# Running sums of log decays made in the projection stage instead of in the heads, in a hybrid GLA/HGRN2 layer

## The chip, the cores and the metric

One core of one Trainium2 chip. The metric is the device time of one launch in microseconds (us); the kernel before takes 1425.37 us, the median of 3 runs (1425.27 to 1426.08). Engines: TensorE (PE in the profile, PEld its weight loads), VectorE (DVE), ScalarE (ACT), GpSimd (POOL), SyncE (SP, which here only issues DMAs).

## The reference, cut to what matters

For a sequence of 1024 positions and width 1024 a projection `p = x @ w_in` makes queries, keys, values, gates and decays. 4 GLA heads (key width 128, value width 256) and 8 HGRN heads (128, 128) each run a linear attention forward and backward. Per direction and head:

```
g = log_sigmoid(lr @ up + bias) / 16            # GLA
g = log(lb + (1 - lb) * sigmoid(h_f))           # HGRN, key = 1 - f
# chunks of 64 positions:
b = cumsum(g, within the chunk)                 # <- what the change moves
o = (q * exp(b)) @ S + masked(q k exp(b_i - b_j)) @ v
S = exp(b_last) * S + (k * exp(b_last - b))^T @ v
```

The outputs of both directions are added, normalised per head, gated, projected (`w_branch_gla`, `w_branch_hgrn`), merged by two sigmoid gates, multiplied by `w_out`, and layer-normed with the residual. All of it is float32.

## The kernel before, in words

The program is written in a tile framework that orders the instructions of each engine itself: it plans with a modelled duration for every instruction and DMA, takes work in the order of the program unless something else is ready earlier, and lets instructions under `high_priority` go first. Each engine and each DMA queue then runs its list strictly in that order. Buffers are tiles with a tag; a tag has a fixed number of buffers, and a new tile waits until the last reader of the tile before it in that buffer is done.

Three stages follow each other; matrix products are made of float32 halves (`split`, lines 88 to 92: a rounded copy on ScalarE, the rest on DVE).

*Stage one* (`dense`, line 1224, about 0 to 711 us) makes all projections by a scheme with seven half-size products in place of eight (`seven`, line 999; the sums of line 1012 run on DVE at high priority). Narrow jobs (TensorE lines 975) make transposed 128-wide pieces: first eight of kind `decay` (`narrow_job`, line 1175), then four `swish`, then `scale` and `copy`; the wide jobs (line 988) make values and gates. While job n runs, the weights of job n + 1 are loaded on SP into `raw` tiles (5 buffers), summed and split. A `decay` job ends with four tiles of 128 x 512 (`h`, 14 buffers), one per head and half: line 1200 makes the key on POOL, line 1202 takes the log on ScalarE in place, line 1203 stores it to the DRAM tensor `logs`. In eight narrow jobs `gla_logs` (line 1159) follows: it makes the GLA logs of one head and direction, 128 x 1024, in two `raw` tiles, the last step on DVE (line 1172), and stores them too. All stores of stage one go out on POOL's queue (`store`, line 920).

*Stage two* (`heads`, line 1471, about 705 to 1213 us) runs the 12 heads in the order of SEQUENCE. `decays` loads a head's logs for both directions into FB and FF (line 1401, 128 x 1024 each, 2 buffers each, on SP). `scaled` (line 1415) makes with a scan on DVE (line 1422) the running sums of the logs into PB and PF (2 buffers each). The scan multiplies the sum so far by `runs`, which is 1.0 everywhere and 0.0 at each 64th position, so that it starts again at every half chunk; direction 1 runs from the right. Then: the last sums of each half chunk are copied to `logs`, a small tile (line 1433), one half is shifted by them (line 1437), two exponentials write FF/FB (line 1440) and PF/PB (line 1441), and these become the scaled key (line 1443) and query (line 1442). `attend` (line 1491) makes the scores (TensorE line 382, masks on DVE lines 392 to 395, with a scratch tile `sq`), transposes the scaled keys (line 540), runs the states (lines 566 and 1568), and ends with the output products `po` (line 566), which read the scaled queries PF and PB and the values `v`. So FF/FB are read until a head's transposes, PF/PB and `v` until its last output products. Projections that the heads don't need (`merge_gate`, `gla_branch`, TensorE line 1364) are given to TensorE between the heads' own products.

*Stage three* (about 1213 to 1425 us) makes the branch projection, the merge and the output; the diff does not touch it.

Of the kernel before, what the change touches and what calls it, by code (L numbers as in the profile page):

```python
# [13 lines left out]
ALU = mybir.AluOpType  # L14
AX = mybir.AxisListType

P = 128
# [857 lines left out]
class Fast(Layer):  # L875
# [283 lines left out]
    def gla_logs(self, h, d):  # L1159

        nc = self.nc
        f, m = self.t("raw"), self.t("raw")
        bias = self.prm[:, 4 * d + h : 4 * d + h + 1]
        for n in range(2):
            o = slice(512 * n, 512 * n + 512)
            ps = self.bank()
            nc.tensor.matmul(ps, self.ups[:, d, P * h : P * h + P], self.lr[:, o], start=True, stop=True)
            nc.scalar.activation(f[:, o], ps, AF.Abs, bias=bias)
            nc.vector.tensor_scalar(out=m[:, o], in0=ps, scalar1=bias, scalar2=0.0, op0=ALU.add, op1=ALU.min)
        nc.scalar.activation(f, f, AF.Exp, scale=-1.0)  # L1170
        nc.scalar.activation(f, f, AF.Ln, bias=1.0)
        nc.vector.tensor_tensor(out=f, in0=m, in1=f, op=ALU.subtract)
        self.store(self.logs[2 * h + d], f)

    def narrow_job(self, kind, at, w):
        nc = self.nc
        late = []

        def out(i, j, _, c, psum):
            s = c if kind == "copy" and not psum else self.h()  # L1180
            col = slice(512 * j, 512 * j + 512)
            if kind == "scale":
                nc.scalar.mul(s, c, QSCALE)
            elif kind != "copy":
                nc.scalar.activation(s, c, AF.Sigmoid)
            elif psum:
                nc.scalar.copy(s, c)
            if kind == "swish":
                nc.vector.scalar_tensor_tensor(out=s, in0=c, scalar=QSCALE, in1=s, op0=ALU.mult, op1=ALU.mult)
            if kind == "decay":  # L1190
                late.append((i, col, s))
            else:
                self.store((self.ks if kind == "copy" else self.qs)[at + i][:, col], s)

        self.seven(self.narrow_product(w, self.xs), 1, out, at == 0 and kind == "decay")
        for i, col, s in late:
            n = HGRN_HEADS * i + at
            o, b = self.omlb[:, n : n + 1], self.lb[:, n : n + 1]
            k = self.h()
            nc.gpsimd.tensor_scalar(out=k, in0=s, scalar1=self.nomlb[:, n : n + 1], scalar2=o, op0=ALU.mult, op1=ALU.add)  # L1200
            self.store(self.ks[GLA_HEADS + n][:, col], k)
            nc.scalar.activation(s, s, AF.Ln, scale=o, bias=b)
            self.store(self.logs[2 * (GLA_HEADS + at) + i][:, col], s)

    def wide_job(self, kind, columns, w):
# [18 lines left out]
    def dense(self):  # L1224
        nc = self.nc
        self.slot, self.stage_one = T, True
        self.counts = {"raw": 5, "s": 3, "w": 8, "h": 14}
        heads = GLA_HEADS + HGRN_HEADS
        self.qs = self.dr.tile([heads, P, T], F32, name="qs")
        self.ks = self.dr.tile([GLA_HEADS + 2 * HGRN_HEADS, P, T], F32, name="ks")  # L1230
        self.logs = self.dr.tile([2 * heads, P, T], F32, name="logs")
        self.sigs = self.dr.tile([16, P, T], F32, name="sigs")
        self.staged = {}
        jobs = []
        for h in range(HGRN_HEADS):
            jobs.append(("decay", h, (H_FF + P * h, H_FB + P * h)))
        for h in range(0, HGRN_HEADS, 2):
            jobs.append(("swish", GLA_HEADS + h, (H_Q + P * h, H_Q + P * h + P)))
        for h in range(0, GLA_HEADS, 2):
            jobs.append(("scale", h, (A_Q + P * h, A_Q + P * h + P)))  # L1240
            jobs.append(("copy", h, (A_K + P * h, A_K + P * h + P)))
        narrow = len(jobs)
        for start, kind, n in ((A_GATE, "gate", 4), (H_GATE, "gate", 4), (A_V, "v", 4), (H_I, "v", 4)):
            for b in range(0, n, 2):
                jobs.append((kind, None, (start + 256 * b, start + 256 * (b + 1))))

        def block(column):
            halves = []
            for n in range(2):
                r = self.t("raw", (P, 4, 256))  # L1250
                nc.sync.dma_start(out=r, in_=self.io["ww"][WIDE.index(column)][:, 4 * n : 4 * n + 4, :])
                halves.append(r)
            return halves

        def prepare(n):
            kind, at, columns = jobs[n]
            if n < narrow:
                return self.pair_sums(self.pair_loads(self.io["wn"], *(NARROW.index(c) for c in columns)))
            a, b = block(columns[0]), block(columns[1])
            return self.sums(a[0], a[1], b[0], b[1], 256)  # L1260

        nc.sync.dma_start(out=self.prm, in_=self.io["prm"])
        ready = self.load_x(lambda: self.pair_loads(self.io["wn"], *(NARROW.index(c) for c in jobs[0][2])))
        self.lower_bounds()
        self.nomlb = self.t("nomlb", (P, 16))
        nc.vector.tensor_scalar(out=self.nomlb, in0=self.omlb, scalar1=-1.0, scalar2=None, op0=ALU.mult)
        for n, (kind, at, columns) in enumerate(jobs):
            ahead = prepare(n + 1) if n + 1 < len(jobs) else None
            if n < narrow:
                self.narrow_job(kind, at, ready)  # L1270
            else:
                self.wide_job(kind, columns, ready)
            if n == narrow - 9:
                self.low_product()
            elif n >= narrow - 8 and n < narrow:
                self.gla_logs(*divmod(n - narrow + 8, 2))
            ready = ahead
        for i in range(self.STARTED, self.BEGUN):
            self.merge_half(i)
# [115 lines left out]

    def decays(self, n):

        fs = []
        for d in (1, 0):
            f = self.t("FB" if d else "FF")  # L1400
            self.nc.sync.dma_start(out=f, in_=self.logs[2 * n + d])
            fs.insert(0, f)
        return fs

    def key(self, n):
        k = self.t("K")
# [5 lines left out]
        self.nc.sync.dma_start(out=q, in_=self.qs[n])  # L1412
        return q

    def scaled(self, q, k, f, unit, d, index):

        nc = self.nc
        pr = self.t("PB" if d else "PF")
        last = 0 if d else 63
        seg = lambda a: a.rearrange("p (s j) -> p s j", j=64)  # L1420
        step = -1 if d else 1
        nc.vector.tensor_tensor_scan(  # L1422
            out=pr[:, ::step],
            data0=self.runs,
            data1=f[:, ::step],
            initial=0.0,
            op0=ALU.mult,
            op1=ALU.add,
        )
        logs = self.t(f"logs{d}", (P, NT, 2))  # L1430
        ends = self.t(f"ends{d}", (P, NT, 2))
        flat = lambda a: a.rearrange("p c h -> p (c h)")
        nc.vector.tensor_copy(out=flat(logs), in_=seg(pr)[:, :, last])
        nc.vector.tensor_reduce(out=self.minp[:, index : index + 1], in_=flat(logs), axis=AX.X, op=ALU.min)
        nc.scalar.activation(flat(ends), flat(logs), AF.Exp, scale=unit)
        half = pr.rearrange("p (c h j) -> p c h j", h=2, j=64)[:, :, d, :]
        nc.vector.tensor_tensor(
            out=half, in0=half, in1=logs[:, :, d].unsqueeze(2).to_broadcast([P, NT, 64]), op=ALU.subtract
        )
        nc.scalar.activation(f, pr, AF.Exp, scale=-unit)  # L1440
        nc.scalar.activation(pr, pr, AF.Exp, scale=unit)
        nc.vector.tensor_tensor(out=pr, in0=pr, in1=q, op=ALU.mult)
        nc.vector.tensor_tensor(out=f, in0=f, in1=k, op=ALU.mult)
        return pr, f, ends
# [26 lines left out]
    def heads(self):  # L1471
        nc = self.nc
        self.oa = self.dr.tile([KC, P, T], F32, name="oa")
        self.oh = self.dr.tile([KC, P, T], F32, name="oh")
        self.ua = self.dr.tile([KC, P, T], F32, name="ua")
        self.runs = self.t("runs")
        nc.vector.memset(self.runs, 1.0)
        nc.vector.memset(self.runs.rearrange("p (s j) -> p s j", j=64)[:, :, 0], 0.0)
        for n, name in enumerate(self.SEQUENCE):
            (self.gla_front if name[0] == "A" else self.hgrn_front)(int(name[1]))  # L1480
            if n == 0:
# [210 lines left out]
    def run(self):  # L1692
        of = lambda *names: [f"{name}{k}" for name in names for k in range(4)]
        with ExitStack() as ctx:
# [3 lines left out]
            with ExitStack() as kept:  # L1698
                self.keep_x = self.pool(kept, "keepx")
                with ExitStack() as c:  # L1700
                    self.tops = self.pool(c, "tops")
                    self.stage(c, "p0", [["raw"], ["s"], ["w"], ["h"]])
                    self.dense()
                with ExitStack() as c:
                    self.stage(
# [6 lines left out]
                            ["Sf", "sq"],  # L1712
                            ["V"],
                            ["FB", "FF"],
                            ["runs"],
                            ["PB", "PF"],
                            ["v"],
                            ["A", "KT", "Sb"],
# [92 lines left out]
```

## Time and profile before

| | |
|---|---|
| median of 3 runs | 1425.37 us |
| the profiled execution | 1426.49 us |
| its span, first to last instruction | 1424.8 us |
| granted TensorE clock, mean over the span | 0.975 of full |
| busy: PE, PEld, DVE, ACT, POOL | 1339.6 (94%), 1152.1 (81%), 862.4 (61%), 670.6 (47%), 182.9 (13%) us |
| chain that ended last, shares | PE 71%, DMA 10%, DVE 7%, ACT 5%, issue 5% |

The profile is one execution; times inside it are us from the first instruction. "Busy" counts the time in which an engine executes something. A timeline row is: start, duration, engine, line of the kernel, operation, written tile <- read tiles, shapes, how many such instructions in a row; in brackets the time the engine stood idle just before, and what ended that. `sc`, `po`, `st`, `proj` and `bank` are PSUM tiles.

### The profile page before, as it was taken

To read this page: it belongs to the slowest core of one execution; us is meant where nothing else is said; L and a number is where in the kernel's file an instruction comes from. 1 tells how busy PE (TensorE), PEld (TensorE's weight loads), DVE (VectorE), ACT (ScalarE), POOL (GpSimd) and SP (SyncE) were. 2 spreads that over 40 slices of the span, in tenths; PEclk is the share of its full clock that TensorE was granted. 3 is DMA by queue.
4 is the path that set the end of the run, shared out by engine and by line. 5 is a ranking of instruction groups with operands and counts; after the bars stand their busy time and mean duration, and the time that the engine had idled before them with its cause. 6 is when DMAs were issued, how large, how long until landed. Compare 5 with 4: busy or idle time off the path is not lost.

```text
span 1424.8 us, 21066 instructions
## 1 busy us (share of the span) xinstructions
PE 1339.6 (94%) x8009; PEld 1152.1 (81%) x8009; DVE 862.4 (61%) x1410; ACT 670.6 (47%) x1190; POOL 182.9 (13%) x270
## 2 busy tenths in 40 slices
PE   7999979999999999999989999987889999799996
PEld 5888858877799999999968877765677888577885
DVE  8755645776566665544463666766788443665544
ACT  6656565774533333222244565556676454653100
POOL 1234350111111011011100010111110100000011
PEclk9999989999999999999999999998899999899998
DMA  7444342333433332332473454355565331865431
GB/s 274 140 148 167 129 151 101 135 138 111 154 131 108 107 102 99 99 114 104 144 278 121 139 185 166 109 177 177 178 231 212 104 112 60 294 231 169 150 103 55
DMA packets 83153, 210.45 MB, mean 148 GB/s; under 512 B 10656, under 2 KB 10656, under 8 KB 80992
## 3 DMA queue, kind: packets, MB, share of 16 engines
q1 hardware_dynamic: 68368, 160.48, 33.1%
q0 software_dynamic: 14672, 48.51, 9.0%
q8 instruction: 65, 1.06, 0.3%
q14 instruction: 48, 0.39, 0.1%
HBM read 137.65 MB, written 71.30 MB: 147 GB/s over the span
## 4 chain that ended last, share of the span: by engine, by line
PE 71%; DMA 10%; DVE 7%; ACT 5%; issue 5%; POOL 0%; SPq 0%; DVEq 0%; POOLq 0%; ACTq 0%
PE bank L988 22%; PE bank L975 16%; PE proj L1364 12%; PE bank L1636 6%; PE po L566 4%; PE st L566 3%; DMA raw<-in_dram 3%; PE sc L382 2%; DMA wraw<-in_dram 2%; PE bank L1304 2%; DMA g<-ua 2%; DMA oa<-ot 1%; PE sc L540 1%; DVE PF L1422 1%; DMA hraw<-oa 1%
## 5 line engine op out<-in xcount | busy, mean ns | idle before, releaser
L975 PE MATMUL bank<-xP,w 128*128 128x512 f32 x1344 | 315.5, 395 | 13.6 <-DVE h L1012 7.0
L988 PEld LDWEIGHTS bank<-w,xP 128*128 128x128 f32 x2688 | 323.5, 192 | 1.1 <-DVE w L92 0.8
L988 PE MATMUL bank<-w,xP 128*128 128x256 f32 x2688 | 323.6, 283 | 0.3 <-DVE w L92 0.3
L975 PEld LDWEIGHTS bank<-xP,w 128*128 128x128 f32 x1344 | 255.1, 190 | 71.4 <-DVE h L1012 8.4
L1364 PE MATMUL proj<-x,hw 128*128 128x512 f32 x576 | 147.1, 399 | 0.1
L92 DVE TENSOR_TENSOR w<-s,w 128x512 fp32r<-128x512 f32 (+1 forms) x96 | 84.0, 877 | 76.3 <-ACT w L91 76.1
L91 ACT CAST w<-s 128x512 fp32r<-128x512 f32 (+1 forms) x96 | 72.6, 760 | 121.7 <-PE bank L988 78.7
L91 ACT CAST w<-raw 128x512 fp32r<-128x512 f32 (+1 forms) x90 | 65.1, 732 | 128.4 <-PE bank L988 67.0
L1364 PEld LDWEIGHTS proj<-x,hw 128*128 128x128 f32 x576 | 104.9, 188 | 21.9 <-issue 0.7
L1364 PE MATMUL proj<-xP,hw 128*128 128x512 f32 x360 | 97.8, 411 | 6.3 <-DVE hw L92 5.5
L1364 PE MATMUL bank<-oh,hw 128*128 128x512 f32 x384 | 93.1, 401 | 9.9 <-ACT hw L91 4.8
L1529 POOL TENSOR_TENSOR rs<-msall,mhalf 128x4 f32<-128x4 f32 (+1 forms) x32 | 43.0, 1343 | 447.2 <-DVE msall L1528 444.5
L1364 PEld LDWEIGHTS bank<-oh,hw 128*128 128x128 f32 x384 | 72.4, 192 | 30.5 <-ACT hw L91 7.9
L1012 DVE TENSOR_TENSOR h<-bank,h 128x512 f32<-128x512 f32 x96 | 65.8, 687 | 45.9 <-PE bank L988 33.4
L92 DVE TENSOR_TENSOR w<-raw,w 128x512 fp32r<-128x512 f32 (+1 forms) x90 | 75.3, 843 | 29.6 <-ACT w L91 29.6
L1364 PEld LDWEIGHTS proj<-xP,hw 128*128 128x128 f32 x360 | 67.2, 193 | 21.9 <-DVE hw L92 6.6
L1012 DVE TENSOR_TENSOR h<-h,bank 128x512 f32<-128x512 f32 x65 | 44.4, 684 | 53.9 <-PE bank L988 28.7
L92 DVE TENSOR_TENSOR hw<-hraw,hw 128x512 fp32r<-128x512 f32 x64 | 43.8, 687 | 42.5 <-ACT hw L91 42.5
L1566 ACT ACTIVATE V<-st,ends 128x128 f32<-128x128 f32 (+1 forms) x168 | 58.6, 414 | 22.5 <-PE st L566 22.2
L566 PE MATMUL st<-v,KT 128*128 128x128 f32 (+1 forms) x336 | 61.0, 323 | 2.6 <-ACT KT L541 1.4
L1304 PE MATMUL bank<-xP,w 128*128 128x512 f32 x216 | 52.3, 404 | 8.0 <-ACT xP L91 6.6
L91 ACT CAST hw<-hraw 128x512 fp32r<-128x512 f32 x64 | 39.6, 618 | 36.9 <-PE proj L1364 25.6
(194 smaller groups left out, 2008.2 us busy)
## 6 DMA issues: line engine op xcount, KB each, us to landing
raw<-in_dram SPq DMA_DIRECT2D x82, 256.0 KB, 3.2
hraw<-in_dram SPq DMA_DIRECT2D x68, 256.0 KB, 3.5
raw<-in_dram SPq DMA_DIRECT2D x33, 512.0 KB, 3.7
ks<-h POOLq DMA_DIRECT2D x40, 256.0 KB, 3.1
K<-ks SPq DMA_DIRECT2D x20, 512.0 KB, 4.9
logs<-h POOLq DMA_DIRECT2D x32, 256.0 KB, 3.7
gated<-h POOLq DMA_DIRECT2D x32, 256.0 KB, 2.7
vd<-h POOLq DMA_DIRECT2D x32, 256.0 KB, 2.7
```

What stands on the lines that cost most here:

```text
L91: nc.scalar.copy(hi, raw)
L92: (lo_engine or nc.gpsimd).tensor_tensor(out=lo, in0=raw, in1=hi.bitcast(F32), op=ALU.subtract)
L382: mm = lambda out, l, r: nc.tensor.matmul(out, l, r, start=True, stop=True)
L566: self.nc.tensor.matmul(out, l, r, start=(i == 0), stop=(i == len(terms) - 1))
L975: self.nc.tensor.matmul(out[0], a[i][:, k, :], b[k][:, j, :], start=(n == 0 and not more), stop=(n == len(terms) - 1), skip_group_check=True,)
L988: self.nc.tensor.matmul(out[c // 2][:, 256 * (c % 2) : 256 * (c % 2) + 256], b[k][:, j, P * c : P * c + P], a[i][:, k, :], start=(n == 0 a ...
L1012: nc.vector.tensor_tensor(out=to[n], in0=one[n], in1=two[n], op=op)
L1304: self.nc.tensor.matmul(ps, w.both[a][:, k, :], xs[k][:, b, :], start=(m == 0), stop=(m == len(terms) - 1))
L1364: nc.tensor.matmul(ps, parts[k][a], self.plain[k, n][:, b, :], start=(m == 0), stop=(m == len(terms) - 1))
L1529: nc.gpsimd.tensor_tensor(out=rs[:, cs], in0=ms, in1=self.mhalf[:, cs], op=ALU.pow)
L1566: nc.scalar.mul(new, u, ends[:, c, near : near + 1])
L1636: nc.tensor.matmul(pss[m], y[:, k, rows], self.wo[k, n][:, j, part], start=(i == 0), stop=(i == len(terms) - 1))
```

## The change

The scan moves to where the logs are made. In stage one a new function `sum_up` runs it in place, 512 columns at a time, on DVE, between the making of the logs and their store; `runs` becomes a tile of 128 x 512 of stage one, made at its start, and `h` has 13 buffers in place of 14. The DRAM tensor `logs` now holds running sums. In stage two the load goes straight into PB and PF, and FB and FF are first written by the exponentials.

```
@@ gla_logs
         nc.vector.tensor_tensor(out=f, in0=m, in1=f, op=ALU.subtract)
+        self.sum_up(f, d)
         self.store(self.logs[2 * h + d], f)
+
+    def sum_up(self, f, d):
+        for n in range(f.shape[1] // 512):
+            u = f[:, 512 * n : 512 * n + 512][:, :: -1 if d else 1]
+            self.nc.vector.tensor_tensor_scan(out=u, data0=self.runs, data1=u, initial=0.0, op0=ALU.mult, op1=ALU.add)
@@ narrow_job
             nc.scalar.activation(s, s, AF.Ln, scale=o, bias=b)
+            self.sum_up(s, i)
             self.store(self.logs[2 * (GLA_HEADS + at) + i][:, col], s)
@@ dense
-        self.counts = {"raw": 5, "s": 3, "w": 8, "h": 14}
+        self.runs = self.t("runs", (P, 512))
+        nc.vector.memset(self.runs, 1.0)
+        nc.vector.memset(self.runs.rearrange("p (s j) -> p s j", j=64)[:, :, 0], 0.0)
+        self.counts = {"raw": 5, "s": 3, "w": 8, "h": 13}
@@ decays
-            f = self.t("FB" if d else "FF")
-            self.nc.sync.dma_start(out=f, in_=self.logs[2 * n + d])
-            fs.insert(0, f)
+            pr = self.t("PB" if d else "PF")
+            self.nc.sync.dma_start(out=pr, in_=self.logs[2 * n + d])
+            sums.insert(0, pr)
@@ scaled
-    def scaled(self, q, k, f, unit, d, index):
-        pr = self.t("PB" if d else "PF")
+    def scaled(self, q, k, pr, unit, d, index):
+        f = self.t("FB" if d else "FF")
-        step = -1 if d else 1
-        nc.vector.tensor_tensor_scan(
-            out=pr[:, ::step], data0=self.runs, data1=f[:, ::step],
-            initial=0.0, op0=ALU.mult, op1=ALU.add,
-        )
@@ heads
-        self.runs = self.t("runs")
-        nc.vector.memset(self.runs, 1.0)
-        nc.vector.memset(self.runs.rearrange("p (s j) -> p s j", j=64)[:, :, 0], 0.0)
@@ run: the pools of stage one and two
-                    self.stage(c, "p0", [["raw"], ["s"], ["w"], ["h"]])
+                    self.stage(c, "p0", [["runs"], ["raw"], ["s"], ["w"], ["h"]])
...
-                            ["runs"],
```

## Rows read from the trace of the kernel before

**Rows 1.** Busy times by stretch: from:to, length, PE, PEld, DVE, ACT, POOL, clock, DMA
```profile
45.00:240.00 195.00, 187.07 (x800) 152.89 (x799) 105.38 (x159) 113.61 (x167) 65.44 (x100) 0.97 0.40 140
240.00:392.00 152.00, 144.81 (x643) 118.38 (x643) 99.29 (x145) 96.57 (x129) 19.95 (x37) 0.98 0.38 133
392.00:711.00 319.00, 319.00 (x2648) 318.58 (x2647) 177.31 (x203) 91.07 (x116) 34.52 (x64) 1.00 0.33 111
711.00:734.00 23.00, 17.78 (x77) 14.12 (x76) 12.85 (x11) 5.12 (x8) 2.16 (x4) 0.96 0.68 260
734.00:880.00 146.00, 144.91 (x918) 118.76 (x918) 95.18 (x191) 80.96 (x174) 9.46 (x8) 0.98 0.45 159
880.00:1100.00 220.00, 191.22 (x1222) 153.24 (x1220) 161.10 (x318) 137.53 (x304) 25.08 (x18) 0.94 0.53 184
1100.00:1213.00 113.00, 112.57 (x713) 96.05 (x714) 50.84 (x112) 56.13 (x142) 6.41 (x4) 1.00 0.28 96
```

**Rows 2.** Line 1422's own row: count, ns least/median/most, first and last start
```profile
L1422 DVE TENSOR_TENSOR_SCAN PB<-runs,FB x12: 2260/2286/2292, 726.4 to 1129.8; 128x1024 f32<-128x1024 f32 x12
```

**Rows 3.** Timeline of TensorE, waits behind DVE in the heads
```profile
733.62 5.41 PE L1364 MATMUL proj<-xP,hw 128*128 128x512 f32 x12 [4.37 <-DVE hw L92]
...
959.23 1.11 PE L540 MATMUL sc<-ident,FB 128*128 128x128 f32 x4 [4.01 <-DVE sq L393]
...
997.74 0.71 PE L540 MATMUL sc<-ident,FB 128*128 128x128 f32 x4 [4.01 <-DVE sq L393]
...
1028.32 0.24 PE L382 MATMUL sc<-PB,FB 128*64 128x64 f32 x1 [1.82 <-DVE sq L393]
```

**Rows 4.** Timeline of DVE at two of the scan pairs
```profile
954.33 2.28 DVE L1422 TENSOR_TENSOR_SCAN PB<-runs,FB 128x1024 f32<-128x1024 f32 x1
...
958.78 0.40 DVE L393 TENSOR_TENSOR sq<-sc,m 128x256 f32<-128x256 f32 x1
...
1054.54 2.28 DVE L1422 TENSOR_TENSOR_SCAN PB<-runs,FB 128x1024 f32<-128x1024 f32 x1
```

**Rows 5.** Busy times by stretch, four short ones behind TensorE's waits
```profile
734.00:740.00 6.00, 6.00 (x17) 4.71 (x17) 6.00 (x21) 5.26 (x9) 0.00 (x0) 0.60 0.77 279
960.00:970.00 10.00, 8.41 (x40) 6.29 (x38) 9.93 (x22) 8.84 (x16) 0.70 (x1) 0.80 0.54 177
998.00:1008.00 10.00, 8.39 (x47) 7.64 (x46) 9.81 (x24) 8.01 (x18) 0.69 (x1) 0.66 0.38 121
1062.00:1075.00 13.00, 8.16 (x72) 6.72 (x70) 12.62 (x28) 9.47 (x17) 1.48 (x1) 0.87 0.77 269
```

**Rows 6.** Timeline of SP: a load of logs, a load of values
```profile
924.53 0.40 SPq L1401 DMA_DIRECT2D FB<-logs  x1
...
954.82 0.32 SPq L1322 DMA_DIRECT2D v<-vd  x1
```

**Rows 7.** DMA issues: what, queue, count, KB each, median us to landing
```profile
FB<-logs SPq DMA_DIRECT2D x12, 512.0 KB, 4.0
FF<-logs SPq DMA_DIRECT2D x12, 512.0 KB, 6.0
```

**Rows 8.** Groups of DVE instructions by form: count, busy us, mean ns, idle
```profile
L1442 DVE TENSOR_TENSOR PF<-PF,Q 128x1024 f32<-128x1024 f32 x12 | 14.6, 1217 | 0.8 <-ACT PF L1441 0.8
...
L1437 DVE TENSOR_TENSOR PF<-PF,logs 128x512 f32<-128x512 f32 x12 | 8.2, 679 | 0.0
```

**Rows 9.** Narrow jobs from 240: TensorE timeline, then a line of DVE's waits
```profile
316.19 4.16 PE L975 MATMUL bank<-xP,w 128*128 128x512 f32 x17 [1.22 <-DVE w L92]
...
388.08 5.49 PE L975 MATMUL bank<-xP,w 128*128 128x512 f32 x12 [2.98 <-DVE h L1012]
...
DVE s L938 <- DMA raw<-in_dram: 12.7, 4, 5.2
```

**Rows 10.** A decay job: DVE behind the logs; line 1200's own row
```profile
159.46 0.69 DVE L92 TENSOR_TENSOR w<-s,w 128x512 fp32r<-128x512 f32 x1 [3.95 <-ACT w L91]
...
L1200 POOL TENSOR_SCALAR h<-h,nomlb,omlb x32: 766/770/1783, 56.4 to 209.6; 128x512 f32<-128x512 f32 x32
```

More of the change, by code (lines that the diff above doesn't have):

```diff
@@ L1396, in decays @@
     def decays(self, n):
-        fs = []
+        sums = []
         for d in (1, 0):
-            f = self.t("FB" if d else "FF")
-            self.nc.sync.dma_start(out=f, in_=self.logs[2 * n + d])
-            fs.insert(0, f)
-        return fs
+            pr = self.t("PB" if d else "PF")
+            self.nc.sync.dma_start(out=pr, in_=self.logs[2 * n + d])
+            sums.insert(0, pr)
+        return sums
     def key(self, n):
@@ L1413, in query @@
         return q
-    def scaled(self, q, k, f, unit, d, index):
+    def scaled(self, q, k, pr, unit, d, index):
         nc = self.nc
-        pr = self.t("PB" if d else "PF")
+        f = self.t("FB" if d else "FF")
         last = 0 if d else 63
         seg = lambda a: a.rearrange("p (s j) -> p s j", j=64)
-        step = -1 if d else 1
-        nc.vector.tensor_tensor_scan(
[L1423 to L1428, printed above, removed]
-        )
         logs = self.t(f"logs{d}", (P, NT, 2))
```

## The prediction

> **What bounds the kernel now.** I read the page first, then busy times by stage, then TensorE's idle times, then what VectorE (DVE) runs just before each of them. By the page TensorE is busy 94% of the span; the 6% it is not are what a change off TensorE can win or lose. The stage table [rows 1] says where they lie. In the first stage's narrow jobs (45 to 392 us) TensorE is idle 7.9 + 7.2 = 15.1 us, in its wide jobs (392 to 711) not at all, at the border of the stages (711 to 734) 5.2 us, in the first heads (734 to 880) 1.1 us, in the middle heads (880 to 1100) 28.8 us. There DVE is busy 161 of 220 us, 73%, more than in the narrow jobs (54% and 65%).
>
> The 24 scans of line 1422 take 2.28 us each (the row is of the PB half; the PF half is alike) [rows 2], 24 x 2.28 = 54.8 us. They come in pairs, one pair a head. TensorE's long waits in the heads [rows 3] are mostly waits for something that stands behind such a pair in DVE's queue. The clearest: the pair runs from 954.33, `sq` of line 393 follows at 958.78 [rows 4], and TensorE, which needs the bank that `sq` reads, starts at 959.23 after 4.01 us of idleness. `sq` belongs to the head before; it waits for no scan by data, only by place. Rows 3 has the same at 997.74 and 1028.32, and at 733.62, where both heads' scans stand ahead of a weight split. Behind the pair of 1054.54 DVE's queue is nearly full until 1075 [rows 4, 5], with 4.84 us of TensorE idleness.
>
> After such idleness TensorE runs slow for a while: of its two levels (1.2 and 2.4 GHz) it is granted the lower for part of each stretch that follows, mean 0.60, 0.80, 0.66 and 0.87 [rows 5].
>
> **Part 1: the scans leave the heads.** Stalls that go: 4.37 + 4.01 + 4.01 + 1.82 [rows 3] and of the 4.84 at 1062 to 1075 about 4.4, the length of the pair: 18.6 us. Lost clock that goes with them [rows 5]: 6 x 0.40 + 10 x 0.20 + 10 x 0.34 + 13 x 0.13 = 9.5 us. Together 28 us. The other pairs lie beside dense TensorE work (734 to 880, and after 1100) and free nothing there. The memset of `runs` in line 1477 goes too; nothing waits for it for long, 0.
>
> What is late next is the part's own new wait. The load of the logs now lands in PF/PB, not in FF/FB. FF/FB are free once a head's transposes are done, so the old load goes out some 30 us ahead of its scan (issued at 924.53, scan at 954.33). PF/PB are read until the head's last output products; only then can the load go out, about when the load of `v`, which is freed by the same products, goes out today, 954.82 [rows 6]. From issue to landing it takes a median of 4.0 us for FB and 6.0 for FF [rows 7], where the pair of scans took 4.5. So the decays of a head are ready 0 to 1.5 us later than now, in ten of twelve heads (the first two find free buffers). The copies of line 1433, the four exponentials on ScalarE and the products behind them wait for it, and whatever stands behind those on the two in-order queues. Cover: DVE has the previous head's mask products, `ss`, `gate` and `A` to do (it is 9.93 of 10 us busy at 960 to 970 [rows 5]). On SP, weight loads, stores of `ot` and K and Q loads stand behind a load that waits. Bounds: 0, and 10 x 1.5 = 15 us; I take the middle, 8, because the two medians lie on both sides of 4.5. Heads: -28 + 8 = -20.
>
> **Part 2: the scans enter the first stage.** No row shows a scan of 512. DVE operations of 512 and 1024 columns take 679 and 1217 ns [rows 8], 0.56 of the long one; a scan of 512 is then between 1.14 (half) and 2.28 us (if length did not matter), and nearest 0.56 x 2.28 = 1.27; I take 1.25. There are 8 x 2 in the low-rank decays and 32 in the jobs of kind decay: 48 x 1.25 = 60 us on DVE.
>
> Low-rank decays (240 to 392): 2.5 us more behind line 1172 in each of 8 blocks, DVE from 99 to 119 of 152 us. Queued behind: weight splits and `h` sums, for which TensorE waits; on the POOL queue the store leaves 2.5 us later, with the stores of `qs` and `ks` behind it, and the `raw` buffer comes free 2.5 us later for the next weight load on SP. Four times in this region DVE stands waiting for a weight load, 12.7 us in all [rows 9], 3.2 each: those blocks hide their scans. Of the other four, TensorE already waits right behind two: 1.22 us at 316.19, 2.98 at 388.08 [rows 9]. Four exposed blocks make 10 us, all eight 20, none 0; since the sums and splits are issued at high priority and may be put ahead of the scans, I take 7.
>
> Decay jobs (the first eight, in 45 to 240): four scans a job, 5 us, behind four Lns of ScalarE. They fall on a DVE that is idle 3.95 us at this place [rows 10] and 46% of the stretch [rows 1]; 1 to 2 us a job spill into the next idle times. Bounds 0 and 8 x 2 = 16; I take 0, since TensorE is busy 187 of 195 and the weights are split a job ahead. The log store on POOL waits up to 5 us longer; behind it stands the next job's line 1200, whose engine is busy 65 of 195 us. One `h` buffer less (13 of 14): a job uses 11 and they are free after their store, 0; without that cover the `h` sums wait out one store, about the 4.0 us of rows 7, a job. The memsets of the shorter `runs` run while the first loads are under way, 0. Wide jobs: TensorE 319.00 of 319 busy, nothing changes.
>
> One rule speaks against the move. In rows 10, line 1200 on POOL takes 770 ns as a rule and up to 1783 where a DVE operation with two SBUF inputs runs. The Trainium skill ("SBUF — State Buffer", section "SBUF: two separate sides") says why: such a DVE operation and a GpSimd operation that reads SBUF take an exclusive lock, and one waits for the whole of the other; the trace's extra 1 us agrees. A scan has two SBUF inputs. In the heads POOL reads little; here line 1200 is next door. I count 0, as POOL is on no path; the case in which it counts is a rival.
>
> **Sum.** -20 + 7 + 0 = -13 us. The profiled execution took 1426.49 us (span 1424.8, 1.7 around it), 1.1 above the median of 1425.37. 1426.5 - 13 - 1.1 = **1412 us**.
>
> **Rivals.** (a) *The load takes the scans' place.* If DVE's copies of line 1433 stand in its queue ahead of the previous head's work, DVE waits for the whole load: ten heads x (0.4 issue [rows 6] + 6.0) = 64 us in place of 10 x 4.5 = 45, +19; no stall goes but that of the border (4.4 + 2.4 of clock), +7 in the first stage: +19, **1445**, slower. It decides from a landing later than the ready work lasts. For it: the order is planned before the run, with a modelled load, and load and products now follow each other. Against: DVE has ready work then, and the decays are needed only a head later.
> (b) *The first stage pays in full.* All eight blocks expose their scans: +20 - 20, **1425**, no change. For it: the waits at 316.19 and 388.08. Against: four idle times of 3.2 us.
> (c) *All of it pays.* The loads hide (8), the blocks hide (7), and half of the other 14.6 us of idleness at 880 to 1100 goes with a shorter queue (7): **1390**. For it: the waits there are of one loop, head after head, that DVE stands in. Against: some of them wait for ScalarE and for loads.
> (d) *The lock counts.* A scan in each job meets a POOL operation and waits its 0.77 us out, 8 x 0.77 = 6 us, all on TensorE's path: 1412 + 6 = **1418**. So far the trace lets POOL and DVE collide without TensorE waiting.
> That the change doesn't do what it says I leave out: each scan starts again at every 64 columns, so 512 at a time are the same sums, and 24 scans must leave the heads.
>
> **How the numbers follow.** Forecast 45% (its own range 1403 to 1421), (a) 20%, (b) 17%, (c) 14%, (d) 4%. No change means within 0.2%, 1422.5 to 1428.2, about what a measurement can tell. Of (b) 5 points fall below, 9 inside, 3 above. Faster: 45 + 14 + 4 + 5 = 68%; same 9%; slower 20 + 3 = 23%. The range 1394 to 1436 leaves out about half of (c) and two thirds of (a), 20%.
>
> **What would show it.** Right: no scan after 711; TensorE goes on at about 729 and not 733.6; no wait of 4 us on `sq` of line 393; granted clock near 1.00 at the places of rows 5; TensorE idle at 880 to 1100 down from 28.8 to about 15; scans of about 1.25 us; 240 to 392 some 7 us longer. Loads of PB and PF go out with or after the last output products and line 1433 follows a landing. Wrong: DVE idle before line 1433, waiting for a load, for more than 1 us a head (a); narrow jobs longer by over 15 us, with TensorE waiting behind line 1172 (b). A new order in which the heads no longer interleave as now would undo the working as a whole.

## The result, and the profile after

The changed kernel takes 1408.15 us, median of 4 runs (1404.65 to 1414.26), beside 1425.72 of the kernel before in the same session: ratio 0.9871, 95% interval 0.9826 to 0.9916. The forecast was 1412. A second set of runs, on another chip, gave 0.9854 (0.9822 to 0.9885). Times and ratios are of the fast runs alone: a run of 4618.48 us, of the version with 13 `h` buffers below, is left out. The profiled execution took 1407.21 us, span 1405.5, mean clock 0.978. The busy times by stretch of the kernel after, to set beside [rows 1]:

```profile
45.00:240.00 195.00, 186.91 (x793) 152.55 (x792) 137.84 (x185) 110.74 (x163) 68.94 (x99) 0.96 0.39 137
240.00:392.00 152.00, 145.87 (x660) 119.20 (x658) 118.06 (x165) 101.53 (x136) 18.91 (x35) 1.00 0.37 130
711.00:734.00 23.00, 22.37 (x110) 18.68 (x109) 6.64 (x16) 5.01 (x9) 2.70 (x5) 1.00 0.69 252
880.00:1100.00 220.00, 199.89 (x1276) 160.57 (x1275) 142.35 (x313) 142.37 (x312) 15.49 (x18) 0.95 0.58 197
```

DVE's work has moved as counted: +32 and +19 us in the two narrow stretches, less in the stretches behind 711. TensorE is idle 20.1 us at 880 to 1100 in place of 28.8. But the work no longer stands in the same microseconds, so the heads have to be cut by their own ends: from the last product of line 988 to the first of line 848, behind the last head. First the kernel before, then after:

```profile
710.90:1221.50 510.60, 471.34 (x2960) 386.12 (x2958) 324.54 (x645) 281.62 (x629) 45.13 (x36) 0.97 0.46 163
```

```profile
714.00:1203.80 489.80, 464.66 (x2961) 381.66 (x2959) 276.19 (x621) 281.74 (x630) 30.56 (x36) 0.98 0.48 166
```

The heads, border included, are 20.8 us shorter: TensorE's idle time falls from 39.26 to 25.14 (-14.1), and the same products (2960 and 2961 records) take 6.7 us less of TensorE's time. Stage one ends 3.1 us later, and what lies behind line 848 takes 1.6 less: +3.1 - 20.8 - 1.6 = -19.3, the difference between the spans.

The scans after, by line, are to be set beside [rows 2] (count, least/median/most ns, first and last start):

```profile
L1180 DVE TENSOR_TENSOR_SCAN h<-runs,h x32: 1197/1200/1226, 69.8 to 217.8; 128x512 f32<-128x512 f32 x32
L1180 DVE TENSOR_TENSOR_SCAN raw<-runs,raw x16: 1199/1208/1224, 249.8 to 391.7; 128x512 f32<-128x512 f32 x16
```

None starts after 391.7. Of [rows 3], the border and the three waits on `sq` have no successor. TensorE goes on at the border at 730.93 (it was 733.62), and at 946.52 it starts the transposes with no wait, since `sq` has been made at once. TensorE's timeline first, then DVE's of the same head:

```profile
730.93 0.73 PE L1375 MATMUL proj<-xP,hw 128*128 128x512 f32 x2 [0.63 <-ACT hw L91]
...
946.52 0.60 PE L540 MATMUL sc<-ident,FB 128*128 128x128 f32 x4
```

```profile
945.99 0.42 DVE L393 TENSOR_TENSOR sq<-sc,m 128x256 f32<-128x256 f32 x1
...
949.16 0.17 DVE L1435 COPY logs<-PB 128x16 f32<-128x16 f32 x1
...
955.70 0.17 DVE L1435 COPY logs<-PF 128x16 f32<-128x16 f32 x1 [2.42 <-DMA PF<-logs]
```

The last row is the new wait: line 1435 (1433 before) copies the ends of the sums once the load has landed. The loads go out on SP with `v`, as they had to:

```profile
945.42 0.32 SPq L1412 DMA_DIRECT2D PB<-logs  x1
946.28 0.32 SPq L1333 DMA_DIRECT2D v<-vd  x1
946.71 0.36 SPq L1412 DMA_DIRECT2D PF<-logs  x1
```

The clock at the four places of [rows 5] is not what it was to be:

```profile
734.00:740.00 6.00, 6.00 (x28) 4.97 (x27) 0.99 (x3) 1.01 (x2) 0.00 (x0) 1.00 1.03 404
960.00:970.00 10.00, 8.86 (x49) 5.76 (x49) 6.54 (x11) 8.89 (x21) 0.00 (x0) 0.75 0.88 328
998.00:1008.00 10.00, 9.82 (x71) 9.15 (x71) 3.50 (x8) 5.01 (x15) 0.00 (x0) 0.77 0.75 254
1062.00:1075.00 13.00, 13.00 (x79) 11.42 (x78) 5.57 (x12) 7.68 (x23) 0.57 (x1) 0.92 0.43 143
```

Only the border is at 1.00; two of the others rose, by 0.11 and 0.05, and one fell by 0.05. Part of this is other work, as the heads run up to 18 us earlier; DVE, 97 to 100% busy at these places before, has room at all four. In the heads TensorE now waits mostly for ScalarE (waited for: us in total, times, longest):

```profile
PE st L566 <- ACT V L1565: 5.1, 7, 1.6
PE po L1539 <- ACT ot L1545: 3.8, 4, 2.3
PE proj L1375 <- ACT hw L91: 3.2, 3, 1.6
```

### The profile page after: what moved, and what is told of

It reads as the page before. It is cut to its first block, busy times and chain, and to the rows that moved or that the text cites. A ratio compares the mean times of both kernels' runs of the same rounds, so it can differ in the third digit from the quotient of the medians.

```text
span 1405.5 us, 21115 instructions
## 1 busy us (share of the span) xinstructions
PE 1333.9 (95%) x8009; PEld 1150.1 (82%) x8009; DVE 867.5 (62%) x1434; ACT 670.9 (48%) x1190; POOL 172.6 (12%) x270
## 4 chain that ended last, share of the span: by engine, by line
PE 74%; DMA 11%; ACT 6%; DVE 5%; issue 3%; POOL 1%; SPq 0%; POOLq 0%; DVEq 0%; ACTq 0%
PE bank L988 22%; PE bank L975 16%; PE proj L1375 13%; PE bank L1635 6%; PE po L566 5%; PE st L566 3%; PE sc L382 2%; DMA raw<-in_dram 2%; PE bank L1315 2%; DMA PF<-logs 2%; DMA hraw<-in_dram 2%; PE bank L1375 2%; DMA g<-ua 1%; DMA g<-sigs 1%; DMA oa<-ot 1%
## 5 line engine op out<-in xcount | busy, mean ns | idle before, releaser
L1375 PE MATMUL proj<-xP,hw 128*128 128x512 f32 x360 | 94.3, 402 | 2.0 <-ACT hw L91 1.6
L1528 POOL TENSOR_TENSOR rs<-msall,mhalf 128x4 f32<-128x4 f32 (+1 forms) x32 | 28.4, 887 | 441.2 <-DVE msall L1527 434.8
```

What stands on the lines that cost most here:

```text
L1375: nc.tensor.matmul(ps, parts[k][a], self.plain[k, n][:, b, :], start=(m == 0), stop=(m == len(terms) - 1))
L1528: nc.gpsimd.tensor_tensor(out=rs[:, cs], in0=ms, in1=self.mhalf[:, cs], op=ALU.pow)
```

## The experiments

The theory: the 24 scans cost time by their place, ahead of the previous head's masks in DVE's queue. The main rival: they cost by DVE's time, wherever they stand. Each ratio is to runs of the kernel before on the same chip, with its 95% interval; versions that ran on different chips are compared by these ratios. "heads" is the stretch of one profile from the last product of line 988 to the first of line 848; before it is 510.6 us.

**The load early again.** The sums are loaded into FF/FB and the query's exponential is the first to write PF/PB:

```
-            pr = self.t("PB" if d else "PF")
-            self.nc.sync.dma_start(out=pr, in_=self.logs[2 * n + d])
+            f = self.t("FB" if d else "FF")
+            self.nc.sync.dma_start(out=f, in_=self.logs[2 * n + d])
... in scaled: copies and shift on f, then
-        nc.scalar.activation(f, pr, AF.Exp, scale=-unit)
-        nc.scalar.activation(pr, pr, AF.Exp, scale=unit)
+        nc.scalar.activation(pr, f, AF.Exp, scale=unit)
+        nc.scalar.activation(f, f, AF.Exp, scale=-unit)
```

> The changed kernel, but the sums are loaded into FF/FB, which come free some 30 us ahead, and PF/PB are first written by the exponential of the query side. Theory (the load that now waits for the last output products is a cost that is still being paid, DVE's 13.9 us of waits for PF's load): about 1400 us, and no wait of line 1435 for a load. Rival one (the loads are covered, the waits fall beside other work): the changed kernel's 1408. Rival two (both exponentials now run one after the other behind PF/PB's release, and ScalarE becomes the late one): 1412 or more.

Measured: 1396.64 us, 0.9778 (0.9756 to 0.9800), heads 481.5. It is the version that beats both kernels. Run again beside two others below:

> e1_prefetch once more, unchanged, beside the two above on one chip: 0.976 to 0.980 if its gain over the changed kernel is real; 0.984 to 0.988 if it was the scatter of one chip.

1398.0 us, 0.9772 (0.9741 to 0.9804), heads 486.0: the gain over the changed kernel is real, its two ratios being 0.008 to 0.010 higher than these two, 11 to 14 us. My reason for it fell, though. DVE waits longer for loads than in the changed kernel. The changed kernel's waits, and then this one's:

```profile
DVE logs L1435 <- DMA PF<-logs: 13.9, 8, 3.2
```

```profile
DVE logs L1435 <- DMA FB<-logs: 19.7, 6, 6.0
DVE logs L1435 <- DMA FF<-logs: 13.4, 8, 4.7
```

What counts is when it waits: 25.0 of these 33.1 us lie before 888, a stretch in which TensorE misses nothing (144.88 of 146 us busy at 734 to 880). In the middle heads DVE's timeline shows the copies of the head that the changed kernel copies at 949.16 and 955.70 some 32 us earlier, 5 of them from an earlier end of stage one, in the head before and away from its end:

```profile
917.11 0.18 DVE L1435 COPY logs<-FB 128x16 f32<-128x16 f32 x1
...
923.58 0.18 DVE L1435 COPY logs<-FF 128x16 f32<-128x16 f32 x1 [0.84 <-DMA FF<-logs]
```

**Scans that nobody needs, in the changed kernel.** Two of 512 columns a head and direction, of the loaded sums, into a tile that nothing reads:

```
+        junk = self.t("junk", (P, 512))
+        for n in range(2):
+            u = pr[:, 512 * n : 512 * n + 512][:, :: -1 if d else 1]
+            nc.vector.tensor_tensor_scan(out=junk, data0=self.ones, data1=u, initial=0.0, op0=ALU.mult, op1=ALU.add)
```

> The changed kernel with two scans of 512 columns per head and direction put back into the heads, on the loaded sums, into a scratch that nobody reads (1.2 us each, 58 us of DVE in all; the output is unaffected). Theory (what cost before was the scans' place in DVE's queue, ahead of the previous head's work): the gain of the heads goes, about 1425 us, with TensorE waiting again behind DVE operations of lines 392 to 395. Rival (what cost was that the exponentials needed the scans' result): nobody needs these, so 1408 to 1412.

1412.55 us, 0.9875 (0.9852 to 0.9898), where my theory said 1425: DVE has the 58 us in the heads again (163 of 220 us busy at 880 to 1100, more than before), and most of the gain stays. The timeline of DVE shows why: these scans become ready only with the late landing, so the masks go ahead of them:

```profile
905.23 0.42 DVE L393 TENSOR_TENSOR sq<-sc,m 128x256 f32<-128x256 f32 x1
...
909.68 1.22 DVE L1433 TENSOR_TENSOR_SCAN junk<-ones,PF 128x512 f32<-128x512 f32 x1 [2.22 <-DMA PF<-logs]
```

By the ratios they cost 1 to 3 us; in its profile, an execution 4 us above the median, the heads are 502.0, 12 longer. The size is not settled between the two.

**The scans at the old place, their result needed by nobody.** The early-load version with 24 scans of 1024 columns from FF/FB into PF/PB, which the exponential then overwrites:

```
+        nc.vector.tensor_tensor_scan(
+            out=pr[:, ::step], data0=self.runs2, data1=f[:, ::step], initial=0.0, op0=ALU.mult, op1=ALU.add
+        )
```

> The kernel of the early loads (sums made in stage one, loaded into FF/FB), with the 24 scans of 1024 columns put back where they were, from FF/FB into PF/PB; the exponential then writes over their result, so nobody reads it (the output is unaffected). Theory, as amended by the idle scans (a scan costs where it is ready as soon as the last output products are done, for there it goes ahead of the masks of lines 392 to 395; not by DVE's busy time): the gain of the heads goes again, ratio to before about 0.995 to 1.00 (1420 to 1428 us), with TensorE's waits of some 4 us on sq of line 393 back. Rival (what counts is that logs, ends and shift need the scans' result): they don't here, so the ratio stays near 0.98.

1433.84 us, 1.0036 (1.0018 to 1.0053), heads 517.7: the whole gain is gone, by the ratios 37 us against the version without them. DVE's timeline has the picture of [rows 4] again, and TensorE's the wait of [rows 3], 4.02 us here as well:

```profile
990.21 2.28 DVE L1431 TENSOR_TENSOR_SCAN PB<-runs,FB 128x1024 f32<-128x1024 f32 x1
992.40 0.14 DVE L1533 TENSOR_SCALAR msall<-ss 128x2 f32<-128x2 f32 x1
992.46 2.28 DVE L1431 TENSOR_TENSOR_SCAN PF<-runs,FF 128x1024 f32<-128x1024 f32 x1
994.66 0.40 DVE L393 TENSOR_TENSOR sq<-sc,m 128x256 f32<-128x256 f32 x1
```

```profile
995.11 1.11 PE L540 MATMUL sc<-ident,FB 128*128 128x128 f32 x4 [4.02 <-DVE sq L393]
```

Not all of the 37 us is the masks' delay. TensorE's waits on `sq`, here first and then in the early-load version without the scans, and ScalarE's waits for the shift here, at 880 to 1100:

```profile
PE sc L540 <- DVE sq L393: 13.5, 4, 6.8
```

```profile
PE sc L540 <- DVE sq L393: 5.4, 4, 2.2
```

```profile
ACT PB L1446 <- DVE FB L1443: 14.8, 5, 4.3
```

Nobody needs these scans' result, but the shift in place writes the tile that they read, and the query's exponential writes the tile that they write: both stand behind them. So the pair delays the next head's exponentials too, and how the 37 us divide is not shown. The version without scans in the heads has waits on `sq` as well, of up to 2.2 us.

**The late load alone.** The kernel before, with the logs loaded into PF/PB and scanned there in place; stage one as it was:

```
-            f = self.t("FB" if d else "FF")
+            pr = self.t("PB" if d else "PF")
... in scaled
-            data1=f[:, ::step],
+            data1=pr[:, ::step],
```

> The kernel before with one edit: logs are loaded into PF/PB and scanned there in place, in the heads; stage one is as before and makes no sums. Theory of the place (the load, which starts only when the last output products are done, lets the masks go ahead of the scans): most of the gain without moving a scan to stage one, ratio about 0.99 (1410 to 1416 us), no waits of 4 us on line 393. Rival of the chain (the scans lengthen the way from load to scores, and now stand behind the load): ratio 1.00 to 1.01. Rival of the changed kernel's authors, so to say (only scans out of the heads help): ratio 1.00.

1414.71 us, 0.9904 (0.9876 to 0.9932), heads 501.0. All 24 scans are in the heads, and two thirds of the gain by the ratio (0.0096 of 0.0146, the changed kernel beside it), half by the heads (9.6 of 20.8), is there. In the head shown the two scans no longer stand together, and a mask goes ahead of each:

```profile
948.38 0.41 DVE L393 TENSOR_TENSOR sq<-sc,m 128x256 f32<-128x256 f32 x1
...
950.33 2.29 DVE L1422 TENSOR_TENSOR_SCAN PB<-runs,PB 128x1024 f32<-128x1024 f32 x1
...
952.59 0.42 DVE L393 TENSOR_TENSOR sq<-sc,m 128x256 f32<-128x256 f32 x1
...
956.22 2.29 DVE L1422 TENSOR_TENSOR_SCAN PF<-runs,PF 128x1024 f32<-128x1024 f32 x1 [0.29 <-DMA PF<-logs]
```

One mask stands behind a single scan here, and TensorE's waits on `sq` come to 1.1 us, where [rows 3] has 4.01 twice and 1.82.

> The changed kernel itself, for comparison on this chip: ratio 0.987 as before. If stage one's scans cost what the run without them said, it stands some 4 us above that run's 0.984.

This is the changed kernel, unchanged, beside it: 1409.66 us, 0.9854 (0.9822 to 0.9885), heads 489.8.

**The scans early.** The kernel before, with the scan in place in FF/FB and the copies, shift and exponentials as in the early-load version, so that it needs only the early load:

```
-            out=pr[:, ::step],
+            out=f[:, ::step],
             data0=self.runs,
             data1=f[:, ::step],
```

> The kernel before with one edit: the scan runs in place in FF/FB, which the load fills some 30 us ahead, and PF/PB are first written by the exponential of the query side; stage one is as before. Theory of the place (scans may stay in the heads, if they are ready early and don't stand between the last output products and the masks): the gain of the early loads without stage one's price, ratio 0.975 to 0.98 (1390 to 1398 us). Rival (DVE's 55 us in the heads cost by themselves): 0.99 or more.

1414.23 us, 0.9894 (0.9870 to 0.9918), heads 499.3: above what my theory gave. No scan stands directly ahead of a mask of line 393 any more; the scans stand among the state updates (line 1568) of the head ahead of theirs. It differs from the early-load version in the scans alone (and their absence in stage one), by 1.2% of the ratios, 17 us. Either DVE's time costs here, or the longer chain from load to exponentials. The next run tells the two apart: the early-load version with scans that nobody needs, ready just as early.

```
+        junk = self.t("junk", (P, 512))
+        for n in range(2):
+            u = f[:, 512 * n : 512 * n + 512][:, :: -1 if d else 1]
+            nc.vector.tensor_tensor_scan(out=junk, data0=self.ones, data1=u, initial=0.0, op0=ALU.mult, op1=ALU.add)
```

> e1_prefetch (0.978) with two scans of 512 a head and direction added, of the sums in FF/FB into a tile that nobody reads; they are ready as early as the scans of e8_scan_early and give DVE the same work, but no later step waits for their result (the shift in place stands behind them on the same engine in any case). If e8 lost its 17 us because DVE had 55 us more to do at places where TensorE's products wait behind it: ratio 0.987 to 0.992 again, with waits of TensorE on A, KT or sq at 880 to 1100. If e8 lost them because its decays come later, a chain from landing through scan to exponentials: 0.976 to 0.982.

1420.37 us, 0.9923 (0.9896 to 0.9951), heads 502.0. So the loss comes without anybody needing the results. At 880 to 1100 this version, and then the one without the scans:

```profile
880.00:1100.00 220.00, 193.21 (x1252) 154.54 (x1251) 166.15 (x341) 147.04 (x324) 20.35 (x18) 0.95 0.54 187
```

```profile
880.00:1100.00 220.00, 201.80 (x1339) 164.69 (x1338) 146.29 (x332) 151.57 (x341) 19.30 (x18) 0.97 0.56 192
```

20 us more on DVE, 8.6 less on TensorE, and no single wait of `sq` over 1.4 us (2.5 without the scans): TensorE's idle time is spread over `KT`, `Sf`, `gate`, `msall`, at most 3.5 us each. ScalarE's waits in the same stretch show what the scans hold up. With them, and then without:

```profile
ACT Sf L1577 <- DVE V L1573: 11.8, 14, 1.6
ACT Sb L1577 <- DVE V L1573: 9.1, 5, 3.2
```

```profile
ACT Sf L1571 <- DVE V L1567: 1.8, 4, 1.1
ACT Sb L1571 <- DVE V L1567: 0.3, 2, 0.2
```

Line 1573 updates the states of the head ahead, which ScalarE then scales for TensorE; on DVE the scans stand between these updates. In the fence behind it, the shift of the scanned head on DVE, and on ScalarE the exponential that needs it:

```profile
934.19 1.22 DVE L1433 TENSOR_TENSOR_SCAN junk<-ones,FB 128x512 f32<-128x512 f32 x1
935.33 0.46 DVE L1573 SCALAR_TENSOR_TENSOR V<-V,tot-1_8382 128x256 f32<-128x256 f32 x1
935.70 1.22 DVE L1433 TENSOR_TENSOR_SCAN junk<-ones,FB 128x512 f32<-128x512 f32 x1
```

```profile
937.81 0.69 DVE L1443 TENSOR_TENSOR FB<-FB,logs 128x512 f32<-128x512 f32 x1
951.29 1.06 ACT L1446 ACTIVATE PB<-FB 128x1024 f32<-128x1024 f32 x1 [0.27 <-PE po L566]
```

So the longer chain is not what holds ScalarE up: the exponential starts 13 us after the shift, when output products free the tile it writes, and at 880 to 1100 ScalarE never waits for the copied ends or the shift, here or with the needed early scans. Place costs again, ahead of state updates in place of masks. That all of the 17 to 22 us come this way is not shown.

**The price in stage one.** The changed kernel without the scans there:

```
-        self.sum_up(f, d)
-            self.sum_up(s, i)
```

> The changed kernel without the scans in stage one: the logs themselves are stored and loaded, so the running sums are left out of what is computed. Theory (the scans cost stage one some 3 us, as the comparison of the profiles has it): 1405, with the narrow jobs ending 3 to 4 us earlier. Rival one (they cost nothing, the later end of the narrow jobs is chance): 1408. Rival two (they delay the raw buffers and the log stores, 7 us or more): 1401 or less.

1406.02 us, 0.9840 (0.9816 to 0.9863), the changed kernel's ratios being 0.9871 and 0.9854. The same with the early load:

> e1_prefetch without the scans of stage one; the logs are left without running sums, so the output is not the reference's. It prices the 58 us of stage-one scans where the heads are at their best. By the term of the prediction (7 us) the ratio is 0.973 against e11's 0.978; if stage one pays in full (20 us), 0.964; if the scans are free there, the same as e11 within 0.002.

1397.81 us, 0.9776 (0.9750 to 0.9803), against 0.9772 with the scans on the same chip. 58 us of scans in stage one cost nothing that these ratios can tell, and they tell some 4 us apart. The stage's ends scatter too much as well: the narrow jobs' last product ends at 393.6, 397.8, 389.8, 391.4, 391.9 and 390.7 us in the six profiles without scans there (mean 392.5) and at 397.9, 392.8, 395.1, 394.4, 394.7, 394.9 and 395.6 in the seven with them (mean 395.0), 2.5 us later; by the last product of line 988 the means are 1.2 us apart, with a scatter of 8 in the first set. One wait of TensorE is sharper, the one at the last low-rank block. It was 2.98 us at 388.08 [rows 9]; in the changed kernel a sum that it needs stands behind the pair of scans on DVE:

```profile
393.53 4.32 PE L975 MATMUL bank<-xP,w 128*128 128x512 f32 x12 [3.85 <-DVE h L1012]
```

```profile
389.97 0.68 DVE L1012 TENSOR_TENSOR h<-bank,h 128x512 f32<-128x512 f32 x1
390.57 2.33 DVE L1180 TENSOR_TENSOR_SCAN raw<-runs,raw 128x512 f32<-128x512 f32 x2
392.81 0.67 DVE L1012 TENSOR_TENSOR h<-bank,h 128x512 f32<-128x512 f32 x1
```

It is 2.93 to 2.98 us in the six profiles without scans there and 3.80 to 3.91 in the seven with them: 0.9 us. TensorE's waits at 238 to 400 together come to 6.6 to 7.3 us in the first set and 7.5 to 7.9 in the second.

**One `h` buffer less**, in the kernel before:

```
-        self.counts = {"raw": 5, "s": 3, "w": 8, "h": 14}
+        self.counts = {"raw": 5, "s": 3, "w": 8, "h": 13}
```

> The kernel before with 13 h buffers in place of 14, nothing else. Theory (a job leaves enough of them free): no change, 1425.5. Rival (the later start of the first narrow job, 45.1 to 47.0 us in the profiles, is the missing buffer): 1427.5, with the first narrow job at 47.

1430.57 us, 1.0015 (0.9997 to 1.0033), heads 511.1: no change, as counted. The first narrow job's long row of products starts at 45.46 (45.14 before, 47.00 in the changed kernel), so the missing buffer doesn't explain the later start.

The versions side by side (a dash: no scans in the heads):

| version | scans in the heads | load into | ratio | heads, us |
|---|---|---|---|---|
| before | 24, ahead of masks | FF/FB | 1 | 510.6 |
| scans at the old place | 24, not needed | FF/FB | 1.0036 | 517.7 |
| scans that nobody needs, early load | 48 short, among state updates | FF/FB | 0.9923 | 502.0 |
| late load alone | 24, behind the landing | PF/PB | 0.9904 | 501.0 |
| scans early | 24, among state updates | FF/FB | 0.9894 | 499.3 |
| scans that nobody needs, changed kernel | 48 short, behind the landing | PF/PB | 0.9875 | 502.0 |
| changed kernel | - | PF/PB | 0.9871, 0.9854 | 489.8, 489.8 |
| load early again | - | FF/FB | 0.9778, 0.9772 | 481.5, 486.0 |

## Why the prediction came out as it did

The forecast was -13 us; the medians of one session differ by 17.6, the profiled spans by 19.3.

**Heads, -20: measured -20.8.** The sum holds, its make-up only in part.
- Stalls 18.6 and clock 9.5, less the new wait of 8. By the heads' windows 14.1 us of idleness and 6.7 of slow products went, net of the wait. The clock's regain was expected at four places; it is seen in full at one, in small part at two and not at the fourth.
- *"It waits for no scan by data, only by place"*: shown. Scans that nobody needs bring a wait of 4.02 us back at the old place, though they hold up the next head's exponentials as well.
- What took the scans out of that place was misread. I put all 28 us down to the scans leaving, and the late load down as a cost only. The late load alone, with the scans still there, gives 10 us (heads) to 14 (ratio): whatever hangs on a later landing can no longer stand ahead of the masks. The scans' leaving gives the remaining 11 (heads) to 7 (ratio); whether as DVE's time or as a shorter way from the landing is not shown. So the two effects don't add: the late load is a gain while the scans stand at their old place and a cost once they are gone.
- The new wait: two estimates meet. Line 1435 waits 13.9 + 0.4 us on DVE, against bounds of 0 and 15, of which I took 8. Its price against an early load is 4 to 8 us by the heads and 11 to 14 by the ratios. But it is not "decays ready 0 to 1.5 us later": the early load makes DVE wait longer (33 us) and is faster. What the timelines show in its place is that copies, shifts and exponentials fall into the busy end of a head instead of the head before and away from its end; that this is the whole price is not shown. With no late load the gross gain of the heads is 25 to 29 us by the windows, near the 28 of the sum: in the prediction's order, scans out first and the load's cost after, the two terms hold by the heads, and only there. The 8 was a middle taken between two bounds, and that it fits is partly luck.

**Stage one, +7: mis-sized.** The one part of it that stands clear of the scatter is the 0.9 us by which TensorE's last wait in this stretch grew; the ends of the stage moved by 1.2 to 2.5 us in the mean of thirteen profiles, within their scatter, and the ratios show 2 to 4 us in one pair and none in the other, within their intervals. A scan of 512 takes 1.20 to 1.21 us (1.25 expected, from the ratio of [rows 8]). The step that failed is "four exposed blocks make 10 us": of the waits in [rows 9] I took each as one that the scan would lengthen by its 2.5 us. The 2.98 grew to 3.85, and no other wait at 238 to 400 is over 1.11, where 1.22 was the longest. DVE's additional 51 us before 392 leave TensorE's busy time in these stretches about as it was (187.1 and 144.8 before, 186.9 and 145.9 after). The reason is not that the sums and splits all go ahead, as I had thought possible: in each of the eight blocks one of them is the first or second operation behind the pair. But TensorE seldom stands waiting for it. The decay jobs cost 0 as forecast; DVE idles there before scans for 9.8 us in all, waiting for ScalarE. The lock of the Trainium skill ("SBUF — State Buffer", section "SBUF: two separate sides") is one between a DVE operation with two SBUF inputs and a GpSimd operation that reads SBUF. The scans gave it no occasion: in the changed kernel's profile no scan runs beside a computing operation of POOL, only beside its stores (line 921). Line 1207 on POOL does have a longer worst case, but beside DVE operations of lines 92, 939 and 962:

```profile
L1207 POOL TENSOR_SCALAR h<-h,nomlb,omlb x32: 767/780/2159, 58.3 to 213.1; 128x512 f32<-128x512 f32 x32
```

Against [rows 10] the median is 10 ns higher and the longest 376.

**The rivals.** (a), the load in the scans' place, did not come: 2.42 us before a copy at 955.70 and 14.3 us in all, not 64, because DVE has the masks to do first, which was the argument against it. (b) is refuted by the two kernels without scans in stage one. (c), 1390, was right that more is to be had, but not from this change: the early load reaches 1396.64. (d) could not come, since no scan met a computing operation of POOL. Of the prediction's signs some failed: DVE's waits before line 1435 come to 1.2 us a head, over the 1 us that was to tell of (a), so that bound was set too low; TensorE's idle time at 880 to 1100 fell to 20.1 us and not 15; the clock came back at one place of four.

**What stays open.** What DVE's time is worth behind the late landing: 5 to 7 us by the ratios (24 needed scans) and 1 to 3 (unneeded), but 11 to 12 by the heads of single profiles; the differences of these ratios are within or near their intervals. How the 37 us at the old place divide between masks and exponentials. And why the clock at the old places recovers only in part.

## What to carry to other kernels

The same 55 to 58 us on one in-order engine cost next to nothing in stage one, 1 to 12 us behind a late landing, 13 to 22 ahead of it among state updates, and 32 to 38 directly ahead of another head's masks: look for what stands behind an instruction in its queue, not for the engine's busy share. A load target decides when a step becomes ready, and so where an order that takes ready work puts it; when an operation moves, try both buffers as the target. And after moving work away, ask whether an early load has been lost with it.

## What was not expected of the hardware

A scan costs by its length at a rate almost the same at both sizes: 1.20 us for 512 columns, 2.29 for 1024, with reversed columns like forward ones (the 32 scans of `h`, half of them reversed, lie between 1197 and 1226 ns). And single executions of one kernel scatter by more than the first three runs showed: those lay within 0.8 us, while on the chips of the experiments the kernel before ranged from 1423.51 to 1437.28; the ratios above come from many runs on one chip for that reason.
